# A hybrid diffusion layer: where the second gate's products, the token blocks and the last columns stand in the order of work

## The chip, the core and the metric

The kernel runs on one NeuronCore of a Trainium2 chip. Its engines are TensorE (PE: matrix products; PEld is its loading of weights), VectorE (DVE), ScalarE (ACT), GpSimd (POOL, here only an issuer of DMAs) and SyncE (SP, an issuer of DMAs). Each engine works its instructions off in program order and waits on semaphores. The metric is the device time of one execution in microseconds (us); lower is better.

## The reference, cut to what matters

One layer works on 512 tokens of width 2048 with a context of 256 tokens: modulation from a conditioning vector, a combined input projection, eight heads of a gated recurrence and eight heads of windowed attention, and then the part that the change touches:

```python
x = x + gt_m * (concat([hg_lat, at_lat]) @ w_out[l])
x = x + gt_f * swiglu(modulate(rms_norm(x, norm_ffn_g[l]), sh_f, sc_f), w_gate_up[l], w_down[l])
# swiglu(h): gate, up = split(h @ w_gate_up); return (silu(gate) * up) @ w_down     D_FF = 5632
# gt_f is one sixth of silu(c) @ w_mod[l] + b_mod[l]
```

All inputs are fp32. The result must keep nearly fp32 accuracy, so the kernel splits each operand into a high part (fp32r, rounded) and a low part (the rest), and forms high by high, high by low and low by high.

## The kernel before, in words

**Output projection.** `proj_a` multiplies eight blocks of 128 rows of the mixed heads (`mT`, split into two parts) with 512 columns of `w_out`; it holds one PSUM bank for each block of 128 tokens. Its loop `s` takes two row blocks at a time: four values of `s` (0, 2, 4, 6) for a pass, and for each token block six products of 512 columns. `Weights` loads the rows of `w_out` in 512 KB pieces on SP's queue (`wr`, three buffers) and splits them ahead on ACT (`wh`) and DVE (`wl`). After the last `s` of a token block, `add_gated` evacuates it: DVE multiplies by the gate (`tm`, one buffer), DVE adds to the residual `x1[j]`, ACT squares and sums. After token block 3, POOL stores `x1[j]` to `x1_d`. The second half of the heads has four passes j = 0 to 3 over the columns. Before, the last one (j = 3) is made as two passes over two token blocks each, and `w_out`'s last columns are loaded and split twice.

**The second gate.** `gt_f` needs `c @ w_mod` for 2048 columns. `gate_rows(k)` makes four products (column groups of the array) for the k-th of 16 blocks of rows (`gw`, 1 MB each, three buffers, loaded by POOL with `gate_load`). A caller's `before(s)` sets where they stand among the projection's products. Before: k = 0 to 3 in pass 2, 4 to 10 in the two halves of pass 3, 11 to 15 behind it. `est.strict` keeps all later instructions in program order on each engine; before, it starts ahead of pass 3.

**Norm and transposes.** Behind the projection DVE forms the reciprocal root mean square and `diag`, a diagonal matrix of it for each token block. `turn(s, h)` multiplies `x1` by `diag` on PE, which transposes and scales four blocks, into one auxiliary PSUM bank; ACT evacuates it with scale and shift into the block tile `xa[s]`.

**FFN by a seven-product scheme.** Each operand is cut in 2 by 2 blocks, and seven products of sums of blocks (Strassen's scheme in Winograd's form) take the place of eight. For the tokens, `a_sums` forms the four sums (`form_sums`), and `form_low` the low parts; the eight token sets of 14 KB per partition stay on chip (`asets`, tags a0 and a1, eight places each). For the weights, `steps` lists 264 steps: 176 up steps (22 groups of 256 columns by 8 steps) and 88 down steps (16 groups). Step i has 42 products (seven products, two halves, three of high and low). `st_load(i)` loads two 256 KB pieces into an `fx` tile, `st_sums` and `st_high` and `st_low` form sums, high parts (`fh`) and low parts (`fl`), each with three places. In iterations 0 to 5 `turn(i + 2, .)` also stands in the step, and before, `xa[s]` takes one of the three `fx` places.

**Evacuation and DRAM.** A group takes seven of the eight PSUM banks. `evac_up` forms the activations and splits them; POOL stores them to `sf_d` (two stores of 896 KB a group), and `reload` brings them back in pieces of 512 and 384 KB for the down steps, at most two per step before. `evac_down` forms four quarters of a 512 by 512 result; `move` stores partial results to `y_d` (adding there), and for the last round (`FIN`) adds `y_d` into the tile by DMA, multiplies by the gate on DVE, adds `x1_d` by DMA and stores to `out`. For the last columns (j = 3), `prepare(3)` does this to the earlier partial sum, and `done` finishes each quarter. `tail` and `moves` are lists of generators which are advanced by one `yield` per step.

Of the kernel before, what the change touches and what calls it, by code (L numbers as in the profile page):

```python
# [9 lines left out]
F32 = mybir.dt.float32  # L10
# [8 lines left out]
P = 128  # L19
D = 2048  # L20
KC = D // P
# [148 lines left out]
def tile_block(ctx: ExitStack, tc: tile.TileContext, x, c, ctx_in, c_ctx, w_mod, b_mod, norm_mix_g,  # L170
# [1254 lines left out]

    def a_sums(xx):
        dve.tensor_tensor(xx[:, 4:6, :], xx[:, 0:1, :].to_broadcast([P, 2, SC]), xx[:, 1:3, :], op=ALU.subtract)
        yield
        dve.tensor_tensor(xx[:, 6, :], xx[:, 5, :], xx[:, 1, :], op=ALU.subtract)
        dve.tensor_tensor(xx[:, 7, :], xx[:, 6, :], xx[:, 3, :], op=ALU.add)  # L1430

# [25 lines left out]
    for k in range(3):  # L1457
        gate_load(k)
    for j in range(3):
# [9 lines left out]
    est.strict = tc  # L1469
    for i in range(3):  # L1470
        st_load(i)
    last = add_gated(gp, 3, True)

    def before(s):
        gate_rows(4 + s // 2)
        if s == 2:
            st_sums(0)
            st_high(0)
        if s == 4:
            st_low(0)  # L1480
        if s == 6:
            st_sums(1)
            st_high(1)

    proj_a(ws, list(range(8)), mT, (0, 1), 512, last, before)

    def before(s):
        if s > 0:
            gate_rows(7 + s // 2)
        if s == 0:  # L1490
            st_low(1)

    proj_a(ws, list(range(8)), mT, (2, 3), 512, last, before)
    for k in range(11, KC):
        gate_rows(k)
# [18 lines left out]
    def turn(s, h):  # L1514

        if s >= 8:
            return
        if h == 0:
            new_set(s)
            xa[s] = est.tile(fx, [P, 8, SC], F32, "fx", "fx", 3)  # L1520
        kc = s + 8 * h
        pt = aux_bank()
        for n, t in enumerate((2, 3, 0, 1)):
            pe.matmul(pt[:, n * P:(n + 1) * P], x1[kc // 4][:, t, (kc % 4) * P:(kc % 4 + 1) * P], diag[:, t, :],
                      start=True, stop=True, skip_group_check=True)
        act.activation(xa[s][:, 2 * h:2 * h + 2, :], pt.rearrange("p (h t) -> p h t", h=2), AF.Identity,
                       bias=ab2[:, 1, kc:kc + 1], scale=ab2[:, 0, kc:kc + 1])

    def form_sums(s):
        if s < 8:  # L1530
            for _ in a_sums(xa[s]):
                pass
            act.activation(sets[s][0][:, 0:3, :], xa[s][:, 1:4, :], AF.Copy)
            act.activation(sets[s][0][:, 3:7, :], xa[s][:, 4:8, :], AF.Copy)

    def form_low(s):
        if s < 8:
            dve.tensor_tensor(sets[s][1], xa[s][:, 1:8, :], sets[s][0].bitcast(F32), op=ALU.subtract)

# [3 lines left out]
    def evac_up(g, banks):  # L1543

        p1, p2, p6, p7, q4, q5, p3 = banks
        e = est.tile(xg, [P, 4, 512], F32, "big", "big", 4)
        r, u0, t, u1 = (e[:, k, :] for k in range(4))
        act.activation(r, p1, AF.Copy)
        yield
        dve.tensor_tensor(u0, p2, r, op=ALU.add)  # L1550
        dve.tensor_tensor(r, p6, r, op=ALU.add)
        yield
        dve.tensor_tensor(t, r, p7, op=ALU.subtract)
        yield
# [11 lines left out]
        sums = a_sums(xx)  # L1566
# [6 lines left out]
        for i, (a, b) in enumerate(((0, 3), (3, 7))):  # L1573
# [11 lines left out]

    def prepare(j):

        gt = est.tile(fx, [P, 512], F32, "gtr", "gtr", 1)
        pool.dma_start(gt, gtf_d[0:1, 512 * j:512 * j + 512].to_broadcast([P, 512]))
        z = None  # L1590
        if j == 3:
            z = zs[0]
            dve.tensor_tensor(z, z, gt[:, None, :].to_broadcast([P, 4, 512]), op=ALU.mult)
            pool.dma_start(z, rows_of(x1_d, j), accum_op=ALU.add)
        prepared[j] = gt, z

    zs = []
    prepared = {}

    def evac_down(j, b, banks):  # L1600
        p1, p2, p6, p7, q4, q5, p3 = (hf(x) for x in banks)
        c = est.tile(xg, [P, 4, 512], F32, "big", "big", 4)
        c11, r, c21, t = (quad(c, h, n) for h, n in ((0, 1), (0, 0), (1, 1), (1, 0)))
        gt, z = prepared[j] if b == FIN else (None, None)

        def done(h, n):
            if z is not None:
                ck = quad(c, h, n)
                dve.tensor_tensor(ck, ck, gt[:, None, SC * n:SC * n + SC].to_broadcast([P, 2, SC]), op=ALU.mult)
                dve.tensor_tensor(ck, ck, quad(z, h, n), op=ALU.add)  # L1610
                sp_q.dma_start(quad(rows_of(out, j), h, n), ck)

        act.activation(r, p1, AF.Copy)
# [3 lines left out]
        yield  # L1617
        dve.tensor_tensor(t, r, p7, op=ALU.subtract)
        done(0, 1)
        yield  # L1620
        dve.tensor_tensor(c21, t, q4, op=ALU.add)
# [3 lines left out]
        done(1, 0)  # L1625
        yield
        dve.tensor_tensor(r, p3, r, op=ALU.add)
        done(0, 0)
        if z is None:
            moves.append(move(j, b, c, gt))  # L1630
        yield

    def move(j, b, c, gt):

        if b < FIN:
            for a in range(4):
# [10 lines left out]
        dve.tensor_tensor(c, c, gt[:, None, :].to_broadcast([P, 4, 512]), op=ALU.mult)  # L1647
        prepare(j + 1)
        pool.dma_start(c, rows_of(x1_d, j), accum_op=ALU.add)
# [5 lines left out]
    def run_step(i, hooks):  # L1655
        u = steps[i]
        ah, al = sets[u.a]
        if u.first:
            n = sum(v.last for v in steps[:i])
            u.banks = [(mm_bank if (n + k) % 2 == 0 else aux_bank)() for k in range(7)]  # L1660
        else:
            u.banks = steps[i - 1].banks
        for k, (fa, fb) in enumerate(PRODUCTS):
            if k in hooks:
                hooks[k]()
            for b in range(2):
                w = [v[:, fb, b * P:(b + 1) * P] if u.up else v[:, fb, :] for v in (u.hi, u.lo)]
                a = [v[:, fa, :] if u.up else v[:, fa, b * P:(b + 1) * P] for v in (ah, al)]
                mm3(u.banks[k][:, b * SC:(b + 1) * SC], *((w, a) if u.up else (a, w)), start=u.first, stop=u.last,
                    first=u.first and b == 0)  # L1670

# [32 lines left out]
    for i, u in enumerate(steps):  # L1704
# [25 lines left out]
        if not u.up and u.b == FIN and u.first:  # L1730
            if u.g == 0:
                prepare(0)
# [55 lines left out]
```

## Time and profile before

| what | value |
|---|---|
| time, median of 3 runs | 2645.55 us (2640.00 to 2646.84) |
| the profiled execution | 2641.55 us, span 2639.8 us |
| mean granted TensorE clock | 0.984 |
| PE busy | 2531.1 us (96%), 17239 instructions |
| DVE busy | 2105.6 us (80%) |
| ACT busy | 1110.5 us (42%) |
| POOL busy | 265.7 us (10%) |
| chain that ended last | PE 68%, DVE 11%, DMA 10%, issue 6% |

The chain is followed back from the last instruction to what released it. PE is busy nearly all of the span, so time is lost or saved in the stretches where it is not: the end of the output projection and the first FFN steps (about 1200 to 1316 us), the first down steps (about 2160 to 2260 us), and the end.

### The profile page before, as it was taken

To read this page: it belongs to the slowest core of one execution; us is meant where nothing else is said; L and a number is where in the kernel's file an instruction comes from. 1 tells how busy PE (TensorE), PEld (TensorE's weight loads), DVE (VectorE), ACT (ScalarE), POOL (GpSimd) and SP (SyncE) were. 2 spreads that over 40 slices of the span, in tenths; PEclk is the share of its full clock that TensorE was granted. 3 is DMA by queue.
4 is the path that set the end of the run, shared out by engine and by line. 5 is a ranking of instruction groups with operands and counts; after the bars stand their busy time and mean duration, and the time that the engine had idled before them with its cause. 6 is when DMAs were issued, how large, how long until landed. Compare 5 with 4: busy or idle time off the path is not lost.

```text
span 2639.8 us, 44545 instructions
## 1 busy us (share of the span) xinstructions
PE 2531.1 (96%) x17239; PEld 2282.7 (86%) x17239; DVE 2105.6 (80%) x3691; ACT 1110.5 (42%) x1801; POOL 265.7 (10%) x466
## 2 busy tenths in 40 slices
PE   7999999999999999997899999999999999999996
PEld 4579877878888887774899999999999998999996
DVE  4467968787788886544898899899998988888886
ACT  4245444446533333323544444444444443343332
POOL 0000010000010211101000000000000023222301
PEclk9999999999999999998999999999999999999998
DMA  9978767662323335655254544544545587787867
GB/s 348 322 231 270 242 212 240 218 218 62 96 83 106 101 114 185 208 207 215 75 160 138 160 146 146 160 142 150 164 128 160 159 265 264 223 245 225 233 179 190
DMA packets 303574, 487.80 MB, mean 185 GB/s; under 512 B 20225, under 2 KB 177058, under 8 KB 300546
## 3 DMA queue, kind: packets, MB, share of 16 engines
q1 hardware_dynamic: 249824, 334.57, 40.0%
q0 software_dynamic: 40160, 137.74, 17.0%
q10 hardware_dynamic: 13378, 12.65, 1.5%
q8 instruction: 135, 2.21, 0.3%
q14 instruction: 77, 0.63, 0.1%
HBM read 413.04 MB, written 71.84 MB: 184 GB/s over the span
## 4 chain that ended last, share of the span: by engine, by line
PE 68%; DVE 11%; DMA 10%; issue 6%; ACT 2%; POOL 1%; SPq 0%; DVEq 0%; ACTq 0%; POOLq 0%
PE mm L131 40%; PE aux L131 28%; DMA m_w<-in_w_mod_dram 3%; DVE big L131 2%; DVE m_acc L131 2%; DVE wl L131 2%; DVE fx L131 1%; DMA wr<-in_w_in_dram 1%; DMA fx<-in_w_down_dram 1%; DMA big<-x_d 1%; DVE fl L131 1%; DVE ce L131 1%; DMA gw<-in_w_mod_dram 1%; DVE a L131 1%; POOL rs_t L131 1%
## 5 line engine op out<-in xcount | busy, mean ns | idle before, releaser
L131 ACT ACTIVATE fh<-fx 128x768 fp32r<-128x768 f32 (+1 forms) x528 | 500.2, 952 | 734.5 <-DVE fx L131 209.8
L131 DVE TENSOR_TENSOR fl<-fx,fh 128x1792 fp32r<-128x1792 f32 (+2 forms) x333 | 543.8, 1635 | 36.3 <-ACT fh L131 34.6
L131 PE MATMUL mm<-a,fh 128*128 128x256 f32 x2464 | 467.2, 283 | 4.8 <-DVE a L131 2.6
L131 PE MATMUL aux<-a,fh 128*128 128x256 f32 x2464 | 466.9, 283 | 1.4 <-ACT fx L131 0.9
L131 DVE TENSOR_TENSOR fx<-fx 128x256 f32<-128x256 f32 (+1 forms) x816 | 417.8, 512 | 57.9 <-DMA fx<-in_w_down_dram 26.3
L131 PEld LDWEIGHTS mm<-a,fh 128*128 128x128 f32 x2464 | 379.6, 188 | 6.0 <-DVE a L131 2.8
L131 PEld LDWEIGHTS aux<-a,fh 128*128 128x128 f32 x2464 | 379.5, 188 | 2.4 <-ACT fx L131 1.1
L131 ACT ACTIVATE wh<-wr 128x512 fp32r<-128x512 f32 x376 | 227.2, 628 | 306.5 <-PE mm L131 181.2
L131 PE MATMUL mm<-a,fl 128*128 128x256 f32 x1232 | 347.2, 282 | 0.0
L131 PE MATMUL aux<-a,fl 128*128 128x256 f32 x1232 | 347.2, 282 | 0.0
L131 DVE TENSOR_TENSOR wl<-wr,wh 128x512 fp32r<-128x512 f32 x376 | 251.2, 685 | 116.0 <-ACT wh L131 115.3
L131 PE MATMUL mm<-wh,hT 128*128 128x512 f32 x896 | 299.8, 404 | 3.8 <-ACT hT L131 2.9
L131 PE MATMUL aux<-fh,a 128*128 128x256 f32 x1232 | 265.5, 283 | 6.4 <-DVE big L131 6.3
L131 PE MATMUL mm<-fh,a 128*128 128x256 f32 x1232 | 265.9, 283 | 3.6 <-DVE big L131 3.5
L131 PE MATMUL mm<-hT,wh 128*128 128x512 f32 x768 | 247.8, 398 | 0.0
L131 PEld LDWEIGHTS aux<-a,fl 128*128 128x128 f32 x1232 | 232.1, 188 | 0.0
L131 PEld LDWEIGHTS mm<-a,fl 128*128 128x128 f32 x1232 | 232.0, 188 | 0.0
L131 PEld LDWEIGHTS mm<-wh,hT 128*128 128x128 f32 x896 | 170.3, 190 | 55.7 <-issue 8.6
L131 PEld LDWEIGHTS aux<-fh,a 128*128 128x128 f32 x1232 | 209.7, 190 | 8.4 <-DVE big L131 7.1
L131 PEld LDWEIGHTS mm<-fh,a 128*128 128x128 f32 x1232 | 210.1, 190 | 4.9 <-issue 2.2
L131 PE MATMUL mm<-wh,mT 128*128 128x512 f32 x512 | 171.4, 406 | 10.7 <-DVE gsig L131 4.0
L131 PE MATMUL mm<-wl,hT 128*128 128x512 f32 x448 | 179.5, 401 | 0.3 <-DVE wl L131 0.3
(280 smaller groups left out, 4088.6 us busy)
## 6 DMA issues: line engine op xcount, KB each, us to landing
fx<-in_w_gate_up_dram SPq DMA_DIRECT2D x352, 256.0 KB, 3.3
wr<-in_w_in_dram SPq DMA_DIRECT2D x144, 512.0 KB, 4.5
m_w<-in_w_mod_dram SPq DMA_DIRECT2D x96, 512.0 KB, 4.7
fx<-in_w_down_dram SPq DMA_DIRECT2D x176, 256.0 KB, 6.7
sf_d<-big POOLq DMA_DIRECT2D x44, 896.0 KB, 5.9
ring<-in_w_mod_dram SPq DMA_DIRECT2D x64, 512.0 KB, 8.9
a<-sf_d POOLq DMA_DIRECT2D x44, 512.0 KB, 11.7
wr<-in_w_out_dram SPq DMA_DIRECT2D x36, 512.0 KB, 4.5
```

What stands on the lines that cost most here:

```text
L131: r = f(*a, **k)
```

## The change

The three `for j` passes and the two half passes become four equal passes; `weave` spreads gate products 0 to 12 over passes 1 to 3 and leaves 13 to 15 behind them; the first weights are loaded in pass 1 and formed in passes 2 and 3; program order is kept from pass 1 on. The block tiles of the first six token sets take places of the set pool in place of `fx`'s. The stores to `sf_d` and `y_d` are issued one step later. `reload` takes two pieces at even steps and one at odd ones. The earlier partial sum of the last columns is prepared by `rest()` from the step after group 2's first of the last round. The last two steps go product by product, and `evac_last` finishes the quarters.

```diff
-        for j in (0, 1, 2, 3, 3) if half else range(4):
+        for j in range(4):
             ws.add(w_out, mix_order[8 * half:8 * half + 8], 512 * j, 512, 2)
...
+    def weave(j, s):
+        if j == 1 and s == 6:
+            for i in range(3):
+                st_load(i)
+        for k in {(1, 0): (0,), (1, 2): (1,), (1, 4): (2,), (1, 6): (3,), (2, 0): (4,), (2, 2): (5,), (2, 4): (6,),
+                  (2, 6): (7,), (3, 0): (8,), (3, 2): (9, 10), (3, 4): (11,), (3, 6): (12,)}.get((j, s), ()):
+            gate_rows(k)
+        for (jj, ss), f, i in (((2, 4), st_sums, 0), ((2, 4), st_high, 0), ((2, 6), st_low, 0), ((3, 0), st_sums, 1),
+                               ((3, 0), st_high, 1), ((3, 2), st_low, 1)):
+            if (jj, ss) == (j, s):
+                f(i)
+    for j in range(4):
         def before(s):
             if j == 0:
                 upto(s + 4)
-            if j == 2:
-                gate_rows(s // 2)
-            if s == 4:
+            weave(j, s)
+            if s == 4 and j < 3:
                 load_gate(gp, j + 1)
+        if j == 1:
+            est.strict = tc
         proj_a(ws, list(range(8)), mT, NT, 512, add_gated(gp, j, True), before)
...
-    proj_a(ws, list(range(8)), mT, (0, 1), 512, last, before)
...
-    proj_a(ws, list(range(8)), mT, (2, 3), 512, last, before)
-    for k in range(11, KC):
+    for k in range(13, KC):
         gate_rows(k)
...
-            xa[s] = est.tile(fx, [P, 8, SC], F32, "fx", "fx", 3)
+            if s < 6:
+                xa[s] = (est.tile(asets, [P, SC], F32, "a1", "xa0", 8), est.tile(asets, [P, 7, SC], F32, "a0", "xa", 8))
+            else:
+                xx = est.tile(fx, [P, 8, SC], F32, "fx", "fx", 3)
+                xa[s] = xx[:, 0, :], xx[:, 1:8, :]
...
-        act.activation(xa[s][:, 2 * h:2 * h + 2, :], pt.rearrange("p (h t) -> p h t", h=2), AF.Identity,
-                       bias=ab2[:, 1, kc:kc + 1], scale=ab2[:, 0, kc:kc + 1])
+        if h == 0:
+            act.activation(x0, pt[:, :SC], AF.Identity, **ab)
+            act.activation(xx[:, 0, :], pt[:, SC:], AF.Identity, **ab)
+        else:
+            act.activation(xx[:, 1:3, :], pt.rearrange("p (h t) -> p h t", h=2), AF.Identity, **ab)
...
+        moves.append(spill(g, hl))
+    def spill(g, hl):
+        yield
+        for i in range(2):
             pool.dma_start(sf_d[2 * g + i].bitcast(F32).rearrange("f p n -> p f n"), hl[i].bitcast(F32))
-            yield
+        yield
...
+    def rest():
+        z = est.tile(xg, [P, 4, 512], F32, "big", "big", 4)
+        pool.dma_start(z, rows_of(y_d, 3))
+        gate_cols(est.tile(asets, [P, 512], F32, "a0", "gt3", 8), 3)
+        yield
+        yield
+        dve.tensor_tensor(z, z, gts[3][:, None, :].to_broadcast([P, 4, 512]), op=ALU.mult)
+        pool.dma_start(z, rows_of(x1_d, 3), accum_op=ALU.add)
+        zs.append(z)
+        yield
...
         if b < FIN:
+            yield
             for a in range(4):
...
-        prepare(j + 1)
+        if j < 2:
+            gate_cols(est.tile(fx, [P, 512], F32, "gtr", "gtr", 1), j + 1)
...
+        if i == len(steps) - 2:
+            return
         for k, (fa, fb) in enumerate(PRODUCTS):
...
+            for u in steps[-2:] if i == len(steps) - 1 else steps[i:i + 1]:
+                for b in range(2):
...
-        for _ in range(2):
+        for _ in range(2 - i % 2):
...
+        if i == len(steps) - 1:
+            evac_last(u.banks)
+            break
...
-        st_low(i + 2, not tail and not g)
+        st_low(i + 2, i >= 8 and not tail and not g)
...
         if not u.up and u.b == FIN and u.first:
...
-            if u.g == 3:
-                zs.append(est.tile(xg, [P, 4, 512], F32, "big", "big", 4))
-                pool.dma_start(zs[0], rows_of(y_d, 3))
+            if u.g == 2:
+                moves.append(rest())
```

## Rows read from the trace of the kernel before

**Rows 1.** Windows: busy PE, PEld, DVE, ACT, POOL (instructions), PEclk, DMA share, GB/s.

```profile
1220.00:1240.00 20.00, 11.64 (x66) 3.99 (x64) 6.12 (x21) 1.45 (x4) 2.35 (x4) 0.75 0.71 258
...
1260.00:1280.00 20.00, 15.72 (x129) 15.30 (x130) 15.86 (x22) 11.20 (x14) 0.00 (x0) 1.00 0.27 80
...
1320.00:1340.00 20.00, 20.00 (x169) 20.00 (x168) 19.06 (x24) 10.11 (x11) 1.52 (x2) 1.00 0.52 168
```

**Rows 2.** Chain that ended last: start us, length us, what; from four places.

```profile
1157.25 1.00 PE aux L131 x8
1158.24 5.67 PE mm L131 x24
...
1317.63 0.72 PE mm L131 x6
...
2153.97 10.36 DMA fx<-in_w_down_dram
```

**Rows 3.** Timeline of PE, 1220 to 1250: start, length, operation, [idle before <-releaser].

```profile
1224.78 0.39 PE L131 MATMUL mm<-wh,mT 128*128 128x512 f32 x1
...
1235.89 1.94 PE L131 MATMUL aux<-gw,c_pad 128*32 128x512 f32 x8 [7.03 <-DMA gw<-in_w_mod_dram]
...
1240.24 4.73 PE L131 MATMUL aux<-diag,x 128*128 128x128 f32 x40
```

**Rows 4.** Timeline of DVE: evacuation of a token block, and the norm's end.

```profile
1184.40 0.69 DVE L131 TENSOR_TENSOR tm<-mm,gt_c 128x512 f32<-128x512 f32 x1 [0.85 <-ACT tm L131]
...
1226.11 0.69 DVE L131 TENSOR_TENSOR tm<-mm,gt_c 128x512 f32<-128x512 f32 x1 [0.85 <-ACT tm L131]
...
1231.58 0.69 DVE L131 TENSOR_TENSOR diag<-ident,rs_y 128x512 f32<-128x512 f32 x1
```

**Rows 5.** Timeline, a transposing step (DVE, ACT, PE, DVE) and PE one later.

```profile
1267.01 2.02 DVE L131 TENSOR_TENSOR a<-fx,a 128x1792 fp32r<-128x1792 f32 x1
...
1269.13 0.78 ACT L131 ACTIVATE fx<-aux,ab 128x512 f32<-128x512 f32 x1 [2.21 <-DVE a L131]
...
1269.96 1.16 PE L131 MATMUL aux<-diag,x 128*128 128x128 f32 x8 [1.41 <-ACT fx L131]
...
1271.96 1.61 DVE L131 TENSOR_TENSOR fx<-fx 128x512 f32<-128x512 f32 x3 [1.42 <-ACT fx L131]
...
1278.44 1.16 PE L131 MATMUL aux<-diag,x 128*128 128x128 f32 x8 [1.40 <-ACT fx L131]
```

**Rows 6.** Waits from 1190 to 1320: total us, times, longest us.

```profile
PE aux L131 <- ACT fx L131: 8.9, 6, 2.4
```

**Rows 7.** Waits from 2150 to 2300: total us, times, longest us.

```profile
PE aux L131 <- DVE big L131: 6.3, 4, 2.4
...
PE mm L131 <- DVE big L131: 3.5, 4, 2.0
```

**Rows 8.** Timeline of POOL's DMA issues in the first down steps.

```profile
2152.10 1.01 POOL L131 DMA_DIRECT2D sf_d<-big  x1 [9.23 <-DVE big L131]
2153.11 6.05 POOL L131 DMA_DIRECT2D a<-sf_d  x8
```

**Rows 9.** Timelines of POOL, DVE and PE at the end.

```profile
2600.44 1.30 POOL L131 DMA_DIRECT2D big<-y_d  x1 [4.08 <-DVE big L131]
...
2609.90 2.29 DVE L131 TENSOR_TENSOR big<-big,gtr 128x2048 f32<-128x2048 f32 x1 [3.47 <-DMA big<-y_d]
...
2616.70 0.28 PE L131 MATMUL aux<-fh,a 128*128 128x256 f32 x1
...
2618.61 2.63 POOL L131 DMA_DIRECT2D big<-x_d  x2 [5.56 <-DVE big L131]
...
2632.49 0.79 POOL L131 DMA_DIRECT2D out_dram<-big  x1 [11.25 <-DMA big<-x_d]
```

**Rows 10.** DMA from 1130 to 1245: GB/s in 40 slices; packets, volume, mean.

```profile
GB/s 24 158 12 218 354 211 143 71 153 32 174 390 422 262 287 274 358 366 407 75 10 311 365 406 387 418 404 243 15 148 219 228 211 291 188 299 430 177 6 3
DMA packets 8278, 26.31 MB, mean 229 GB/s; under 512 B 720, under 2 KB 2256, under 8 KB 6608
```

More of the change, by code (lines that the diff above doesn't have):

```diff
@@ L1458, in tile_block @@
         gate_load(k)
-    for j in range(3):
+    def weave(j, s):
[10 more added lines that the diff above has]
+    for j in range(4):
         def before(s):
@@ L1525, in turn @@
                       start=True, stop=True, skip_group_check=True)
-        act.activation(xa[s][:, 2 * h:2 * h + 2, :], pt.rearrange("p (h t) -> p h t", h=2), AF.Identity,
-                       bias=ab2[:, 1, kc:kc + 1], scale=ab2[:, 0, kc:kc + 1])
+        ab = dict(bias=ab2[:, 1, kc:kc + 1], scale=ab2[:, 0, kc:kc + 1])
+        x0, xx = xa[s]
+        if h == 0:
[3 more added lines that the diff above has]
+            act.activation(xx[:, 1:3, :], pt.rearrange("p (h t) -> p h t", h=2), AF.Identity, **ab)
     def form_sums(s):
         if s < 8:
-            for _ in a_sums(xa[s]):
+            for _ in a_sums(*xa[s]):
                 pass
-            act.activation(sets[s][0][:, 0:3, :], xa[s][:, 1:4, :], AF.Copy)
-            act.activation(sets[s][0][:, 3:7, :], xa[s][:, 4:8, :], AF.Copy)
+            act.activation(sets[s][0][:, 0:3, :], xa[s][1][:, 0:3, :], AF.Copy)
+            act.activation(sets[s][0][:, 3:7, :], xa[s][1][:, 3:7, :], AF.Copy)
     def form_low(s):
         if s < 8:
-            dve.tensor_tensor(sets[s][1], xa[s][:, 1:8, :], sets[s][0].bitcast(F32), op=ALU.subtract)
+            dve.tensor_tensor(sets[s][1], xa[s][1], sets[s][0].bitcast(F32), op=ALU.subtract)
     def hf(bank):
@@ L1565, in evac_up @@
         dve.tensor_tensor(xx[:, 1:4:2, :], hf(r), hf(u0), op=ALU.mult)
-        sums = a_sums(xx)
+        sums = a_sums(xx[:, 0, :], xx[:, 1:8, :])
         next(sums)
@@ L1572, in evac_up @@
         yield
-        for i, (a, b) in enumerate(((0, 3), (3, 7))):
+        for a, b in ((0, 3), (3, 7)):
             dve.tensor_tensor(hl[1][:, a:b, :], xx[:, 1 + a:1 + b, :], hl[0].bitcast(F32)[:, a:b, :],
                               op=ALU.subtract)
+            yield
[3 more added lines that the diff above has]
+        for i in range(2):
             pool.dma_start(sf_d[2 * g + i].bitcast(F32).rearrange("f p n -> p f n"), hl[i].bitcast(F32))
-            yield
+        yield
     def rows_of(d, j):
@@ L1584, in quad, with gate_cols, parts_of @@
         return c[:, 2 * h:2 * h + 2, SC * n:SC * n + SC]
[L1586 to L1598, printed above, removed]
+    def gate_cols(t, j):
+        pool.dma_start(t, gtf_d[0:1, 512 * j:512 * j + 512].to_broadcast([P, 512]))
+        gts[j] = t
+    def rest():
[8 more added lines that the diff above has]
+        yield
+    gts, zs = {}, []
+    def parts_of(c):
+        return [quad(c, h, n) for h, n in ((0, 1), (0, 0), (1, 1), (1, 0))]
     def evac_down(j, b, banks):
@@ L1602, in evac_down @@
         c = est.tile(xg, [P, 4, 512], F32, "big", "big", 4)
[L1603 to L1611, printed above, removed]
+        c11, r, c21, t = parts_of(c)
         act.activation(r, p1, AF.Copy)
@@ L1618, in evac_down, with evac_last, done @@
         dve.tensor_tensor(t, r, p7, op=ALU.subtract)
+        yield
+        dve.tensor_tensor(c21, t, q4, op=ALU.add)
+        dve.tensor_tensor(t, q5, t, op=ALU.subtract)
+        dve.tensor_tensor(r, q5, r, op=ALU.subtract)
+        yield
+        dve.tensor_tensor(r, p3, r, op=ALU.add)
+        moves.append(move(j, b, c))
+        yield
+    def evac_last(banks):
+        p1, p2, p6, p7, q4, q5, p3 = (hf(x) for x in banks)
+        c = est.tile(xg, [P, 4, 512], F32, "big", "big", 4)
+        c11, r, c21, t = parts_of(c)
+        def done(h, n):
+            ck = quad(c, h, n)
+            dve.tensor_tensor(ck, ck, gts[3][:, None, SC * n:SC * n + SC].to_broadcast([P, 2, SC]), op=ALU.mult)
+            dve.tensor_tensor(ck, ck, quad(zs[0], h, n), op=ALU.add)
+            sp_q.dma_start(quad(rows_of(out, 3), h, n), ck)
+        act.activation(r, p1, AF.Copy)
+        dve.tensor_tensor(c11, p2, r, op=ALU.add)
         done(0, 1)
-        yield
+        dve.tensor_tensor(r, p6, r, op=ALU.add)
+        dve.tensor_tensor(t, r, p7, op=ALU.subtract)
         dve.tensor_tensor(c21, t, q4, op=ALU.add)
@@ L1656, in run_step @@
         u = steps[i]
-        ah, al = sets[u.a]
         if u.first:
@@ L1665, in run_step @@
                 hooks[k]()
[L1666 to L1670, printed above, removed]
+            for u in steps[-2:] if i == len(steps) - 1 else steps[i:i + 1]:
+                for b in range(2):
+                    w = [v[:, fb, b * P:(b + 1) * P] if u.up else v[:, fb, :] for v in (u.hi, u.lo)]
+                    a = [v[:, fa, :] if u.up else v[:, fa, b * P:(b + 1) * P] for v in sets[u.a]]
+                    mm3(u.banks[k][:, b * SC:(b + 1) * SC], *((w, a) if u.up else (a, w)), start=u.first,
+                        stop=u.last, first=u.first and b == 0)
     uses = {}
```

38 lines of the change are left out of this document (8 added, 30 removed).

## The prediction

> **What bounds the kernel now.** I read the windows first, in stretches of 50 and then 20 us, since PE is busy 96% of the span and only the stretches where it is not can pay. Three fall out. From 1220 to 1240 us PE has 11.64 of 20 us and a mean granted clock of 0.75; from 1260 to 1280 it has 15.72; from 1320 on it is full [rows 1]. The chain of waits tells what a full stretch costs: one `s` of a pass with four token blocks takes 5.67 us, a gate row 1.00, and six FFN products 0.72, so the 42 of a step take 5.04 us [rows 2]. Third, PE's timeline shows why the first stretch is empty: the projection's last product ends at 1225.2 us, a gate row behind it starts after 7.03 us of waiting for its 1 MB load, and the transposes start only at 1240.24 [rows 3]. DVE does not hold them: `diag` is done at 1232.3, and the last token block's evacuation started at 1226.1; within a pass one starts every 2.26 us (from the one at 1182.14 to that at 1184.40), because ACT gives `tm` back late [rows 4]. Fourth, the step with transposes turns in a ring of four: `form_low` of the set before ends on DVE, then ACT may write the shared `fx` place, then PE gets the one free bank for the second transposes (waits 1.41 us), then ACT, then DVE forms the sums; from one such wait to the next are 8.48 us [rows 5], and the six waits of this kind make 8.9 us [rows 6]. In the first down steps PE waits for DVE's evacuation, 9.8 us in all [rows 7]; DVE itself was late because a weight load took 10.36 us [rows 2], and that load met a burst: POOL stood 9.23 us at a store to `sf_d` and then issued eight reloads in 6.05 us [rows 8]. At the end PE is done at 2617.0, but the group before is multiplied by its gate at 2609.9, after its `y_d` addition; then come the last gate columns and the old partial sum's product, at 2618.6 the two additions of `x1_d`, and at 2632.5 the last 1 MB store, which sets the end at 2639.8 [rows 9].
>
> **Term 1, the passes.** Pass 2 began with its gate row at 1157.25 [rows 2], so pass 1 began 4 x 5.67 earlier, at 1134.6. Three passes of 12 values of `s` with 13 gate rows take 12 x 5.67 + 13 x 1.00 = 81.0 us and end at 1215.6. Before they ended at 1225.2 with 11 rows in them, so 11.6 us were waits or half-speed products. What goes: four loads of 512 KB, eight splits on ACT and on DVE (not on the bound; with two token blocks per `s` they came twice as often as PE could use them). What is added: the three weight loads, their sums and parts (DVE about 3.6 us a step, from 1.6 us of sums and 2.0 of low parts [rows 5]), now behind a full `s` of 6.67 us and covered by splits that are made two values of `s` ahead. Program order from pass 1 on puts four evacuations (4 x 2.26 = 9.0 us, starting when the first block is ready) ahead of the next pass's splits; these end some 6 us into the pass and are needed after 5.67 + 1.00 + half a microsecond. Tight, so I leave 2 us of waits: the end is 1217.6, gain 7.6. Bounds: 9.6 if none, nothing if all the old waits come back.
>
> The stretch's loads are the test of it. Before, 26.31 MB moved in 115 us, mean 229 GB/s, with slices of 366 to 430 GB/s [rows 10]. The new 81 us need 26.3 less 2.1 (the second load of the last columns) and 1.05 (the fourth `x1_d` store falls behind), plus 1.05 for weights loaded early as their places come free: 24.2 MB, 299 GB/s. The Trainium skill ("DMA: Bandwidth & Descriptors", Specifications) gives an HBM limit per core of about 358 GB/s; by it alone the 24.2 MB would take 68 us, so the passes would still be PE's. This case's slices go beyond the figure, and the measurement decides.
>
> **Term 2, the hold before the transposes.** Before: 1240.2 - 1225.2 = 15.0 us [rows 3]. After: blocks are ready every 5.67 / 4 = 1.42 us but evacuated every 2.26, so the last starts at -3 x 1.42 + 3 x 2.26 = 2.5 us behind the end; from there to `diag`'s end was 1232.3 - 1226.1 = 6.2 us [rows 4]: 8.7. Three gate rows (3 us) lie inside it, and the last one's load is issued 5.7 us before the end, so even a 9 us landing is covered. Gain 6.3. Without that cover it is what it was: bound 0.
>
> **Term 3, a cold start.** PE now idles some 5.7 us between gate row 15 and the first transposes. After 7.03 us of idling a gate row took 1.94 us instead of 1.00 [rows 2, 3], the lower of the two clock levels; those slow rows stood ahead of the transposes, whose 40 products then took 4.73 us at the upper one [rows 3]. If half of them run slow that costs 2.4 us, on the path, for ACT needs all four banks before the first high parts. The evacuation in two instructions where there was one of 0.78 us [rows 5] costs between nothing and 0.78 each; I take 0.4 for the ones on the path. Loss 2.8; bounds 0 and 4.7 + 0.8.
>
> **Term 4, the transposing steps.** Own places remove the wait of ACT for `form_low`, so the first transposes' bank is free before PE comes back for it. Without the 1.41 us a step is 8.48 - 1.41 = 7.07 us of PE work; DVE's is the same period less its own wait of 1.42, 7.06 [rows 5]. They balance, so nearly all of the 8.9 us goes [rows 6]; I take 8. Bounds: 3 (DVE and ACT bind at 8 us a step) and 8.9. The last two blocks still use `fx`, in steps where a free place is waiting two us earlier.
>
> **Term 5, the down steps.** The later stores and the slower reload change the order in POOL's queue, not what is moved. POOL is not paced by steps: behind the last store it waits for, it issues everything up to the next. Counting the new list, eleven pieces (not eight) run ahead of the two `sf_d` stores, and behind these come two stores and seven pieces, 4.6 MB, where before one store and eight pieces came, 4.6 MB as well [rows 8]. So the burst stays, and with it DVE's lateness. I take 1 us gain; bounds 9.8 us and a few of clock gained [rows 7], and 5 lost (more pieces ahead of the first weights). Reloads come at the latest five steps, 25 us, before use, hence cost nothing; the held `big` places come free about a step before the next group needs them; the low part in one piece instead of two changes no path.
>
> **Term 6, the end.** `rest` takes the gate columns, the multiplication (2.29) and the first addition out of the end, to step 256. There DVE has 2.3 us more; queued behind are the product of group 1, the next sums and group 2's evacuation, so that chain is 2.3 us later. In the old trace's time: `y_d` addition issued at 2600.4 + 2.3, landing after 9.5, multiplied by 2614.5; the `x1_d` addition (as long as that of `y_d`, 9.5) and 0.3 of issue to 2624.3; the store, from issue to the span's end 7.3 as before, and 0.3 to 2631.9 [rows 9]. The last group is done earlier: 15 DVE instructions of 512 columns from 2614.5, each 0.69 [rows 4], reach 2624.9, and then only 256 KB are left to store, against 1 MB. So the order by product earns nothing by itself: cover is that chain. Gain 7.9, less 1 for weight loads that meet two additions at once: 7. Bounds 3 and 10.
>
> **Sum.** 7.6 + 6.3 - 2.8 + 8 + 1 + 7 = 27.1 us. The profiled execution took 2641.55 us, so 2614.5; it lies 4.0 below the median of 2645.55, from which the sum gives 2618.4. I predict 2616 between them.
>
> **Rivals.** (a) The moved stores do cure the down steps, all of 9.8 us: 2607. For it: POOL's 9.23 us stand and the eight loads behind it; against: the count of term 5. (b) The loads bind the passes. At the old mean of 229 GB/s 24.2 MB take 106 us: the end comes at 1240, term 1 turns from 7.6 gained to 15 lost, and the time is 2616 + 22.6 = 2639; from about 220 GB/s downwards, 110 us, it is slower than before, 2645 and more. Against it: slices of 366 to 430 GB/s in the same stretch, and 20 us of lead for each load. At a mild form, 6 us of waits, 2622. (c) DVE or ACT binds the transposing steps at 8 us: 2621. (d) The clock stays low through all transposes, 4.7 in place of 2.4: 2618. The Trainium skill ("TensorE: Matmul & The Clock Gate", Part 1) says that the clock follows how busy PE was just before, which speaks against leaving PE without gate rows there; the 1.94 us row agrees. (e) The passes stay as late as they were and nothing else counts: within 0.3%.
>
> **Chances and range.** 0.3% (7.9 us) is about what a measurement of this kernel can tell from no change. Forecast 0.50; (a) 0.18; (b) 0.12, of which slower 0.04 and the same 0.03; (c) 0.10; (d) 0.07; (e) 0.03. Faster 0.90, same 0.06, slower 0.04. The range takes (a) with its clock and the upper bounds of terms 4 and 6 at the one end, 2599, and the mild form of (b) together with (c) and the lower bound of term 6 at the other, 2631.
>
> **What would show it.** Right: pass 3's last product near 1217, transposes near 1226, no PE wait of 1.41 us for ACT in steps of about 7.1 us, the full stretch beginning near 1290 instead of 1316, PE still waiting for DVE around the first down groups, and and PE's last product some 15 us before the end instead of 22.8, with the 1 MB store of group 2 as the last to land. Wrong: weight waits in passes 1 to 3, a step of 8 us or more, down steps without waits, or an end set by the last quarters.

## The result, and the profile after

The changed kernel takes 2615.01 us (median of 4 runs, 2612.90 to 2616.42) where the kernel before, run beside it, takes 2642.78 (2639.81 to 2646.84): ratio 0.9893, 95% interval 0.9875 to 0.9912. Forecast were 2616 us and faster. The profiled execution took 2616.11 us, span 2614.3.

Medians of two kernels that differ by 3 us can't be told apart here, but the spans can be cut where PE's timeline has a mark, and the pieces repeat far better. The table has the start of pass 1 (before it nothing was changed; for the old passes it is the first gate row less four values of `s`), the time from there to the second product of step 0 (the row with 2.60 us of waiting for DVE `a`; 2.62 before), from there to the end of the last product, and what follows it. The starts spread over 6.9 us, in code that all kernels share; within one version of a stretch, the second and third columns agree to about 1 us (1.5 with paced reloads), while the last one spreads from 11.8 to 14.8 us over the nine kernels that have the changed kernel's end. The lower twelve kernels are the experiments below. The kernel before took 2636.76 to 2642.78 us beside the different groups of them, so they are compared by the ratio and by the columns, not by their times.

| kernel | pass 1 starts | to step 0's second product | to the last product's end | behind it | ratio to before |
|---|---|---|---|---|---|
| before | 1134.6 | 114.2 | 1368.2 | 22.8 | |
| after | 1132.6 | 101.9 | 1365.0 | 14.8 | 0.9893 [0.9875, 0.9912] |
| u_passes | 1127.7 | 117.4 | 1364.9 | 13.1 | 0.9953 [0.9938, 0.9969] |
| u_places | 1131.7 | 99.8 | 1372.5 | 14.4 | 0.9913 [0.9896, 0.9929] |
| u_down | 1127.9 | 101.6 | 1364.6 | 11.8 | 0.9899 [0.9881, 0.9917] |
| u_end | 1128.8 | 101.7 | 1362.9 | 23.0 | 0.9930 [0.9915, 0.9945] |
| x_warm | 1130.7 | 101.0 | 1363.9 | 11.8 | 0.9893 [0.9876, 0.9910] |
| x_row | 1133.1 | 100.9 | 1364.9 | 13.6 | 0.9908 [0.9890, 0.9926] |
| x_row_warm | 1129.4 | 98.4 | 1363.9 | 12.1 | 0.9889 [0.9868, 0.9910] |
| x_paced | 1131.3 | 101.6 | 1357.6 | 13.0 | 0.9880 [0.9863, 0.9898] |
| x_end2 | 1132.3 | 101.8 | 1372.7 | 7.4 | 0.9911 [0.9896, 0.9926] |
| x_noorder | 1130.2 | 101.6 | 1364.2 | 14.5 | 0.9911 [0.9885, 0.9936] |
| x_best | 1131.2 | 98.4 | 1365.2 | 7.4 | 0.9881 [0.9866, 0.9896] |
| x_warm_paced | 1128.8 | 98.4 | 1359.1 | 12.2 | 0.9862 [0.9845, 0.9878] |

Of the 25.5 us between the two spans, 2.0 are the start's scatter, 12.3 lie in the first stretch, 3.2 in the second and 8.0 behind the last product.

The windows of the kernel after, with the columns of [rows 1]:

```profile
1220.00:1240.00 20.00, 12.87 (x67) 12.35 (x68) 10.65 (x21) 8.38 (x13) 1.95 (x4) 0.67 0.11 41
...
1260.00:1280.00 20.00, 18.23 (x154) 17.98 (x153) 17.93 (x24) 13.96 (x18) 0.00 (x0) 1.00 0.17 53
...
1320.00:1340.00 20.00, 20.00 (x169) 19.96 (x168) 16.64 (x22) 7.86 (x10) 1.01 (x1) 1.00 0.44 140
```

The transposing steps are now 91% full (18.23 of 20 us, 15.72 before). The chain that ended last shows passes at their floor and, later, two slow weight loads (15.10 and 11.93 us):

```profile
1186.96 5.67 PE mm L131 x24
1192.63 1.85 PE aux L131 x16
...
2117.95 15.10 DMA fx<-in_w_gate_up_dram
...
2138.24 11.93 DMA fx<-in_w_down_dram
```

The chain before had two at this place as well, the 10.36 us of [rows 2] and, ahead of it, one of 12.40:

```profile
2131.64 12.40 DMA fx<-in_w_gate_up_dram
```

The timelines of PE, DVE, POOL and ACT between the projection and the first FFN step:

```profile
1213.13 0.39 PE L131 MATMUL mm<-wh,mT 128*128 128x512 f32 x1
...
1222.54 7.10 PE L131 MATMUL aux<-diag,x 128*128 128x128 f32 x40 [6.31 <-issue]
...
1234.47 0.58 PE L131 MATMUL mm<-a,fh 128*128 128x256 f32 x1 [2.60 <-DVE a L131]
...
1216.28 0.69 DVE L131 TENSOR_TENSOR tm<-mm,gt_c 128x512 f32<-128x512 f32 x1 [0.85 <-PE aux L131]
...
1221.75 0.69 DVE L131 TENSOR_TENSOR diag<-ident,rs_y 128x512 f32<-128x512 f32 x1
...
1223.33 1.95 POOL L131 DMA_DIRECT2D gtf_d<-g_row  x4 [4.57 <-DVE g_row L131]
...
1227.41 3.27 ACT L131 ACTIVATE xa<-aux,ab 128x256 f32<-128x256 f32 x6 [8.90 <-DMA gtf_d<-g_row]
```

The projection ends 81.0 us after pass 1 began, and the transposes start 9.0 us later. Two things are new: the 40 transposes take 7.10 us (4.73 in [rows 3]), at a granted clock of 0.67 in that window, and ACT can write the first block only when four stores of the gates' sum `g_row` have landed. The new places for blocks lie on memory that `g_row` had.

A transposing step, by DVE's `form_low` and PE's one remaining wait, and PE's waits for evacuations from 2090 to 2300:

```profile
1251.48 2.02 DVE L131 TENSOR_TENSOR a<-xa,a 128x1792 fp32r<-128x1792 f32 x1
...
1258.40 2.02 DVE L131 TENSOR_TENSOR a<-xa,a 128x1792 fp32r<-128x1792 f32 x1
...
1275.41 1.16 PE L131 MATMUL aux<-diag,x 128*128 128x128 f32 x8 [1.76 <-ACT fx L131]
```

```profile
PE aux L131 <- DVE big L131: 5.7, 4, 4.3
...
PE mm L131 <- DVE big L131: 3.9, 3, 2.0
```

A step takes 6.92 us, and the one wait of the old kind belongs to block 7, which still uses `fx`. In the down steps 9.6 us of waits stand where 9.8 stood [rows 7]. The window begins earlier than that of [rows 7] because these steps now come some 16 us earlier; before, it holds the same 9.8. POOL's issues there, and POOL, DVE and PE at the end:

```profile
2136.39 1.00 POOL L131 DMA_DIRECT2D sf_d<-big  x1 [13.55 <-DVE big L131]
2137.39 4.57 POOL L131 DMA_DIRECT2D a<-sf_d  x6
...
2563.98 1.30 POOL L131 DMA_DIRECT2D big<-x_d  x1 [11.01 <-DVE big L131]
...
2566.83 1.27 POOL L131 DMA_DIRECT2D big<-x_d  x1
2582.65 0.80 POOL L131 DMA_DIRECT2D out_dram<-big  x1 [14.54 <-DMA big<-x_d]
2583.43 1.32 POOL L131 DMA_DIRECT2D big<-y_d  x1
...
2594.84 2.29 DVE L131 TENSOR_TENSOR big<-big,gtr 128x2048 f32<-128x2048 f32 x1 [5.50 <-DMA big<-y_d]
...
2599.24 0.28 PE L131 MATMUL aux<-fh,a 128*128 128x256 f32 x1
...
2606.96 0.79 POOL L131 DMA_DIRECT2D out_dram<-big  x1 [8.23 <-DMA big<-x_d]
```

The end is group 2's chain, read upwards: the 1 MB store at 2606.96 waits for the `x1` addition, that for DVE's product at 2594.84, that for the `y_d` addition, which POOL issued only at 2583.43, behind the store of group 1 for which it stood 14.54 us. Last, the DMA view of the passes, 1130 to 1215 us:

```profile
DMA packets 7876, 24.18 MB, mean 284 GB/s; under 512 B 576, under 2 KB 3136, under 8 KB 6208
```

### The profile page after: what moved, and what is told of

Read it like the earlier page. It is cut to its first block, busy times and chain, and to the rows that moved or that the text cites. A ratio compares the mean times of both kernels' runs of the same rounds, so it can differ in the third digit from the quotient of the medians.

```text
span 2614.3 us, 44525 instructions
## 1 busy us (share of the span) xinstructions
PE 2525.6 (97%) x17239; PEld 2284.1 (87%) x17239; DVE 2098.8 (80%) x3676; ACT 1106.5 (42%) x1801; POOL 265.1 (10%) x466
## 4 chain that ended last, share of the span: by engine, by line
PE 71%; DVE 11%; DMA 9%; issue 5%; ACT 2%; POOL 1%; SPq 0%; DVEq 0%; ACTq 0%; POOLq 0%
PE mm L131 42%; PE aux L131 29%; DMA m_w<-in_w_mod_dram 4%; DVE m_acc L131 2%; DVE fx L131 1%; DVE big L131 1%; DVE wl L131 1%; DMA wr<-in_w_in_dram 1%; DVE fl L131 1%; DVE ce L131 1%; DMA fx<-in_w_down_dram 1%; DMA fx<-in_w_gate_up_dram 1%; DVE a L131 1%; DMA io<-mix_d 0%; POOL rs_t L131 0%
## 5 line engine op out<-in xcount | busy, mean ns | idle before, releaser
L131 DVE TENSOR_TENSOR fx<-fx 128x256 f32<-128x256 f32 (+1 forms) x798 | 408.5, 512 | 52.7 <-DMA fx<-in_w_down_dram 26.0
L131 ACT ACTIVATE wh<-wr 128x512 fp32r<-128x512 f32 x368 | 221.6, 627 | 290.1 <-PE mm L131 153.8
L131 DVE TENSOR_TENSOR wl<-wr,wh 128x512 fp32r<-128x512 f32 x368 | 245.2, 685 | 101.4 <-ACT wh L131 100.6
L131 PE MATMUL aux<-fl,a 128*128 128x256 f32 x616 | 173.8, 282 | 0.0
## 6 DMA issues: line engine op xcount, KB each, us to landing
a<-sf_d POOLq DMA_DIRECT2D x44, 512.0 KB, 11.4
a<-sf_d POOLq DMA_DIRECT2D x44, 384.0 KB, 11.4
```

Source lines behind the costliest of these rows:

```text
L131: r = f(*a, **k)
```

## The experiments

**The four parts undone, one at a time.** Each kernel is the changed one with one part put back as the kernel before has it: u_passes the two half passes with the gate rows' places, the late loading of the first weights and program order only behind the third pass, u_places the blocks in `fx`, u_down the stores to `sf_d` and `y_d` and two reloads a step, u_end the old preparation of the last columns and the last two steps one after the other.

```diff
 u_passes
-        for j in range(4):
+        for j in (0, 1, 2, 3, 3) if half else range(4):
 u_places
-            if s < 6:
-                xa[s] = (est.tile(asets, ...), est.tile(asets, ...))
+            xa[s] = est.tile(fx, [P, 8, SC], F32, "fx", "fx", 3)
 u_down
-            yield
-        moves.append(spill(g, hl))
+            pool.dma_start(sf_d[2 * g + i]..., hl[i]...)
+            yield
...
-        for _ in range(2 - i % 2):
+        for _ in range(2):
 u_end
-            if u.g == 2:
-                moves.append(rest())
+            if u.g == 3:
+                zs.append(est.tile(xg, [P, 4, 512], F32, "big", "big", 4))
+                pool.dma_start(zs[0], rows_of(y_d, 3))
...
-            evac_last(u.banks)
```

> The changed kernel with the old passes: last columns in two half passes, the second gate's products as before with five behind the projection, program order only from there. Theory (terms 1 to 3): the projection ends 9 to 10 us later, the transposes start 15 instead of 9 us behind it, and the first transposes are warm again (4.7 instead of 7.1 us): 11 to 15 us in all, time 2626 to 2630. Rival (the old waits were the chip's DMA rate and would show in the one-pass form as well): less than 5 us.

> The changed kernel with the token blocks back in the fx places and their evacuation in one instruction. Theory (the ring of four waits, term 4): PE waits for ACT's evacuation again in six steps, some 8 us in all, against the one of 1.8 us that is left in the changed kernel; steps of 8.5 us again. But ACT's first evacuation then no longer waits for the store of the second gate (8.9 us of idling in the changed trace, behind memory that its new place shares), so some 2 us come back: time 4 to 7 us above the changed kernel's 2615.0, 2619 to 2622. Rival (DVE or ACT would bind these steps anyway): less than 2 us.

> The changed kernel with the stores to sf_d and y_d at their old steps and two reload pieces at each step again. Theory (term 5: the same bursts in another order): PE's waits for DVE's evacuation in the first down steps stay between 7 and 11 us (9.8 before, 9.0 after), and the time stays within 3 us of 2615.0. Rival (a) (the moved stores cure these waits, and something else hid it): 6 to 10 us more.

> The changed kernel with the old end: the last columns' old partial sum prepared behind the group before, the last two steps one after the other. Theory (term 6): PE's last product to the end of the span 22 to 23 us instead of 14.8, PE itself about 1 us earlier, time 2621 to 2623. Rival (the order by product is what shortens the end): with the order undone, PE's end to the last quarter's store alone would grow, and the time by 2 to 5 us only.

u_passes: 2625.55 us, and the first stretch 15.5 us longer than in the changed kernel, a little over the 11 to 15 expected. The transposes run fast again (the first 32 take 4.85 us), but the first step does not gain by it: from the transposes to the second product it still takes 11.7 us, for ACT still waits for the store of `g_row` (its first block at 1238.08, 16.54 us idle, ended by that store). Its PE timeline has the split's late high parts and the gate row's late load back:

```profile
1199.91 0.80 PE L131 MATMUL mm<-wh,mT 128*128 128x512 f32 x1 [2.39 <-ACT wh L131]
...
1229.10 1.93 PE L131 MATMUL aux<-gw,c_pad 128*32 128x512 f32 x8 [7.14 <-DMA gw<-in_w_mod_dram]
```

u_places: 2615.91 us. The ring is back, with steps of 8.42 us (DVE's rows) and a wait of 1.33 to 2.00 in each of four (6.0 us in all; some 8 in six were expected), 7.5 us in the second stretch. But the first stretch is 2.1 us shorter: ACT starts 2.1 us after PE's first transposes (1223.74 after 1221.65), with no store ahead of it. The columns give 5.4 us together, within the 4 to 7 expected; the intervals of the two ratios overlap.

```profile
1258.00 2.02 DVE L131 TENSOR_TENSOR a<-fx,a 128x1792 fp32r<-128x1792 f32 x1
...
1266.42 2.02 DVE L131 TENSOR_TENSOR a<-fx,a 128x1792 fp32r<-128x1792 f32 x1
...
1269.37 1.16 PE L131 MATMUL aux<-diag,x 128*128 128x128 f32 x8 [1.33 <-ACT fx L131]
```

u_down: 2610.73 us, and 1364.6 against 1365.0 us: the later stores and the slower reloads are worth nothing that shows. PE's waits from 2090 to 2300 are 8.4 us (5.9 and 2.5), within the 7 to 11 expected. POOL's burst is there in both (here eight reloads in 6.03 us at 2128.10).

u_end: 2619.45 us. Behind the last product 23.0 us are back, as expected, in the old form: DVE's product waits for the gate columns, and both additions of `x1` come after it.

```profile
2592.16 2.29 DVE L131 TENSOR_TENSOR big<-big,gtr 128x2048 f32<-128x2048 f32 x1 [3.75 <-DMA gtr<-gtf_d]
...
2594.89 2.62 POOL L131 DMA_DIRECT2D big<-x_d  x2 [5.62 <-DVE big L131]
2608.67 0.79 POOL L131 DMA_DIRECT2D out_dram<-big  x1 [11.16 <-DMA big<-x_d]
```

Its second stretch is 2.1 us shorter, so the new end costs PE something; rows name 0.68 and 0.50 us of waits for DVE at 2577 in the changed kernel and 0.50 at 2572 here, the rest is within what that column scatters.

**The first step: a slow clock, or the store?** x_warm adds six rows of products that nobody uses ahead of the transposes, x_row puts the gates' sum into a place of its own, x_row_warm does both.

```diff
 x_warm (behind gate row 15)
+    idle = aux_bank()
+    for n in range(6):
+        for j in range(4):
+            pe.matmul(idle[32 * j:32 * j + 32, :], c_pad[:, 15, :], w15[:, 512 * j:512 * j + 512], ...)
 x_row
-    dve.tensor_tensor(g_row, pg[0], g_row, op=ALU.add)
+    g_sum = est.tile(fx, [P, 512], F32, "fl", "g_sum", 3)
+    dve.tensor_tensor(g_sum, pg[0], g_row, op=ALU.add)
```

> The changed kernel with six more gate rows of idle products (into a bank that nothing reads) between the last gate row and the first transposes, so that PE idles less than 1 us there. Theory (cold start, and behind it a second wait that the prediction had not seen: ACT's first evacuation stands 8.9 us until the second gate's stores have landed, because its place shares memory with their source): the 40 transposing products take 4.7 us instead of 7.1, but ACT still starts at the same time, so that the first step begins at most 1 us earlier; time 2614 to 2615. Rival (the cold start alone holds the first step): 2.4 us earlier.

> The changed kernel with the second gate's sum formed in a free place for low parts, so that no token block's place shares memory with the source of its stores. Theory: ACT's first evacuation follows PE's first transposes at once (no wait of 8.9 us), and with the transposes still cold the first step begins 1 to 2 us earlier; time 2613 to 2614. Rival (the store's wait is hidden behind the cold transposes): no change of the first step.

> Both edits together. Theory: the two waits stand one behind the other and each hides part of the other, so that both together bring more than the sum of each: from the first transposes to the first step's second product 9 us instead of 11.9, the first step 3 us earlier, time 2612. Rival (they add up): the sum of the two single gains.

The times are 2610.09, 2613.86 and 2607.60 us, too near each other for their intervals; the stretch from the first transposes to step 0's second product decides: 11.9 us in the changed kernel, 11.0, 10.9 and 8.4 here. PE's timelines of x_warm and x_row with ACT's of x_row, then of x_row_warm:

```profile
1220.62 3.81 PE L131 MATMUL aux<-diag,x 128*128 128x128 f32 x32 [1.14 <-issue]
...
1225.65 1.16 PE L131 MATMUL aux<-diag,x 128*128 128x128 f32 x8 [1.22 <-ACT xa L131]
```

```profile
1223.09 7.19 PE L131 MATMUL aux<-diag,x 128*128 128x128 f32 x40 [6.29 <-issue]
...
1225.22 1.02 ACT L131 ACTIVATE xa<-aux,ab 128x256 f32<-128x256 f32 x2 [6.16 <-PE aux L131]
```

```profile
1219.37 4.70 PE L131 MATMUL aux<-diag,x 128*128 128x128 f32 x40 [1.15 <-issue]
...
1227.80 0.39 PE L131 MATMUL mm<-a,fh 128*128 128x256 f32 x1 [2.60 <-DVE a L131]
```

With idle products the transposes run fast, but PE then waits for a bank that ACT has not emptied. ACT starts only at 1224.57, 3.95 us after PE; its row names PE, but the chain of this run shows the store just ahead of it:

```profile
1222.86 1.53 DMA gtf_d<-g_row
```

With the store out of the way ACT starts 2.1 us after PE, but PE is slow. Each hides the other: without the store the slow clock costs 2.5 us (10.9 against 8.4), at the higher clock the store costs 2.6 (11.0 against 8.4). Both gone give 3.5 us, where the single ones add up to 1.9.

**The burst of reloads.** x_paced issues the reloads of the stationary sets on ACT's queue, each a step later than the place's last use, in the order of the steps instead of behind a waiting POOL.

```diff
-            if not parts or due[parts[0]] > i or uses[parts[0][0] - 8][-1] > i:
+            if not parts or due[parts[0]] > i or uses[parts[0][0] - 8][-1] >= i:
-            pool.dma_start(sets[n][k].bitcast(F32)[:, f0:f1, :],
+            act.dma_start(sets[n][k].bitcast(F32)[:, f0:f1, :],
```

> The changed kernel with the reloads issued from ACT's queue in place of POOL's, one step later than a set's last use, so that ACT's own work in each step spaces them out and no store stands ahead of them. Theory (term 5: bursts of reloads delay the weight loads, DVE comes late, PE waits for its evacuation and then runs at the lower clock level): no weight load over 8 us in the first down steps, PE's waits there fall from 9.0 to under 3 us, time 2603 to 2609. Rival (DVE's own work in these short groups is the bound, the loads come late for nothing): waits of 6 us or more stay, time above 2611. Second rival: issuing on ACT delays its evacuations, and the time rises.

2606.37 us, and the second stretch 7.4 us shorter (5.9 in x_warm_paced below). Three rows of PE's windows, 2100 to 2200 us (busy PE, granted clock, DMA share, GB/s), of after, u_down and x_paced, the DMA view's line for the down weights (time from issue to landing last), 2100 to 2160, of after and x_paced, and PE's waits in x_paced from 2090 to 2300:

```profile
2100.00:2200.00 100.00, 91.18 (x718) 0.93 0.75 254
```

```profile
2100.00:2200.00 100.00, 92.45 (x732) 0.95 0.87 295
```

```profile
2100.00:2200.00 100.00, 95.81 (x779) 0.97 0.81 270
```

```profile
fx<-in_w_down_dram SPq DMA_DIRECT2D x12, 256.0 KB, 9.1
```

```profile
fx<-in_w_down_dram SPq DMA_DIRECT2D x14, 256.0 KB, 4.3
```

```profile
PE aux L131 <- DVE big L131: 2.7, 2, 2.2
PE mm L131 <- DVE big L131: 2.4, 2, 2.0
```

Weight loads land in half the time, and PE's waits in the first down steps fall from 9.6 to 5.1 us. Less than 3 us were expected, so about half of the waits have another cause, which no run here shows. The rest of the gain stands in no wait; the granted clock over the 100 us is 0.97 in the place of 0.93. Which of the two edits does more was not separated. The Trainium skill ("DMA: Bandwidth & Descriptors", Issuing engines are not separate DMA queues) says that DMAs of all issuers run on the same 16 engines. It agrees with the long loads beside POOL's burst, and by it another queue as such would not make the loads faster; no run here tries it alone.

**The end.** x_end2 finishes the third group of columns in place as well, as the change does the fourth. x_noorder takes the order by product out of the last two steps and leaves all else.

```diff
 x_end2
+            if u.g == 1:
+                moves.append(rest(2, 3))
             if u.g == 2:
-                moves.append(rest())
+                moves.append(rest(3, 0))
...
+        own = j == 2 and b == FIN
+        if own:
+            done(c, j, 0, 1)
+            done(c, j, 1, 1)
 x_noorder
-        if i == len(steps) - 2:
-            return
...
-            for u in steps[-2:] if i == len(steps) - 1 else steps[i:i + 1]:
+            for u in steps[i:i + 1]:
```

> The change kept; in addition the third group of columns is finished by VectorE in place too, from a sum prepared beforehand (its gates loaded, the old partial sum read, multiplied and x1 added while the products run), and SyncE stores its quarters: no block load, no accumulating transfer and no add of 1 MB is left in the last 40 us except the second group's. Theory A (the 14.8 us behind the last product in the changed kernel are the accumulating chain of the third group, y_d added, then x_d added, then the out store on POOL's queue, and VectorE's last pass that waits 5.50 us for it): the end behind the last product falls to about 8 us, the time by 5 to 7 us. Rival B (VectorE's own last passes, some 8 us of rows, set the end, or its extra passes make the products wait): the end stays at 13 us or more and the time within 2 us of the changed kernel's.

> The change kept, but the last two down steps run one after the other again, each over all seven products, as before the change. Theory A (what is left behind the last product is set by the accumulating chain of the group of columns ahead, not by the last block's own evacuation): the time stays within 1 us of the changed kernel's, and the end behind the last product stays at 13 to 15 us, or shows the chain a little longer while the wait on it goes. Rival B (the order by product lets VectorE take the first products' sums while the last ones run, and is what won most of the end): the end behind the last product grows by 4 us or more and the time with it.

x_end2: 2613.08 us. The end behind the last product is 7.4 us as theory A has it, but the second stretch is 7.7 us longer, as B has it. DVE's and PE's timelines show the first piece of that:

```profile
2543.45 2.29 DVE L131 TENSOR_TENSOR big<-big,gt 128x2048 f32<-128x2048 f32 x1 [2.26 <-issue]
...
2547.91 0.44 PE L131 MATMUL aux<-fh,a 128*128 128x256 f32 x1 [3.71 <-DVE big L131]
```

The preparation falls between the pieces of the evacuation of the group before. DVE stands idle (the chain has the preparation's `y_d` load there, 14.58 us from 2527.81) and then multiplies, and PE waits 3.71 us; 1.04, 1.15 and 0.98 follow at 2580 to 2597. These make 6.9 us where the changed kernel has 1.2; the other 2 us were not traced. x_noorder: 2611.16 us and 14.5 us behind the last product, with the same chain on the same waits:

```profile
2591.11 2.29 DVE L131 TENSOR_TENSOR big<-big,gtr 128x2048 f32<-128x2048 f32 x1 [5.27 <-DMA big<-y_d]
...
2603.06 0.79 POOL L131 DMA_DIRECT2D out_dram<-big  x1 [8.07 <-DMA big<-x_d]
```

The 14.5 lie within the spread of the kernels that keep the order (11.8 to 14.8), so the order by product earns nothing that shows.

**Together.** x_best has the own place, the idle products, the paced reloads and x_end2's end; x_warm_paced leaves that end out.

> The change kept, with four additions: the gates' sum in a place of its own, six idle products ahead of the first transposes, the stationary reloads one step later on ScalarE's queue, and the third group of columns finished in place. If the parts add up: the first two gave 4.8 us together (ratio 0.9889 against 0.9893 or 0.9908 alone), the later reloads 5.7 us, the end 5 to 7 us, so 2595 to 2600 us where the changed kernel takes 2612 to 2615. If the late reloads or the extra passes of VectorE meet at the end (both fall in the down steps), the last two are worth less than 8 us together, and the time is 2600 us or more.

> The change kept, with three additions and without the third group's finish in place: the gates' sum in a place of its own, six idle products ahead of the first transposes, and the stationary reloads one step later on ScalarE's queue. Theory (the three act in stages far apart, 900 us, and each stands on the path that sets the end): the trace shows the first transposes to the second product in 8.4 us, from full blocks to the last product 1295.5 us, and 13 us behind the last product; the time is the sum, 4.8 + 5.7 us under the changed kernel, that is a ratio of 0.985 to 0.9865 to the kernel before, 2601 us where the changed kernel takes 2612. Rival (the late reloads' gain was the run's own scatter, as the 1303.0 to 1304.3 us from full blocks to the last product of other runs may be): that stretch is again 1301 us or more and the ratio 0.987 to 0.989.

x_best takes 2606.07 us, not the 2595 to 2600 of parts that add up: x_end2's end takes the paced reloads' gain back (1365.2 us in the second stretch). x_warm_paced takes 2601.24 (2600.24 to 2601.85), ratio 0.9862, within its expected band; both gains stand in their own columns of the table, 3.5 us in the first stretch and 5.9 in the second. Its interval meets those of x_paced, x_row_warm and x_best and just touches the changed kernel's, so that it is the fastest of them rests on the columns as well as on the ratio.

## Why the prediction was right

The total was forecast at 27.1 us. The spans differ by 25.5, of which 2.0 are scatter ahead of the change, so the change itself made 23.5 in these traces; the medians differ by 27.8. That the time lies within 1 us of 2616 is luck in part. Up to the full stretch the terms hold in sum, 19.1 forecast and 18.7 measured. Behind it 8 were forecast and 4.7 came, and the scatter of the start gave 2.0 back. Term by term:

- **Term 1**, forecast 7.6, measured 9.6: 90.6 us of passes before, 81.0 after, the upper bound. The 2 us of waits that I left for the evacuations did not come. 24.18 MB moved, as counted (24.2), at 284 GB/s over a slightly longer window, so rival (b) fell: in the passes no wait of PE for a weight is left.
- **Term 2**, forecast 6.3, measured 6.1: the hold is 9.0 us, by the evacuations' rhythm (the last one starts at 1216.28, 2.8 us behind the passes; forecast 2.5).
- **Term 3**, forecast -2.8, measured -3.4 (8.56 to 11.93 us). The size is near and the reasons are only half right: about half the transposes ran slow, as taken, 7.10 in place of 4.73 us (6.13 to 7.65 in the other runs that idle as long), but the store of `g_row` ahead of ACT was not seen. The two overlap: the slow clock by itself costs 2.5 us, close to the 2.4 taken, and the store puts 1.0 on top of it (x_warm, x_row and x_row_warm). The 0.4 for ACT's evacuation in two instructions does not show: with both causes gone this piece takes 8.4 us, 8.6 before. The Trainium skill ("TensorE: Matmul & The Clock Gate", Part 1) says that the clock follows how busy PE has been; the traces agree: the same 40 products took 7.10 us behind 6.31 us of idling and 4.70 behind 1.15. Rival (d), all 40 slow, is out.
- **Term 4**, forecast 8, measured 6.4 (from step 0's second product to the first full stretch 67.2 us before, 60.7 after) and 7.5 in u_places' column. Steps take 6.92 us (forecast 7.07), so rival (c) is out; what is missing is the wait of 1.76 us of block 7, which I had counted as gone.
- **Term 5**, forecast 1, is nothing: u_down shows it, and the waits stay (9.6 us after 9.8). Eleven pieces run ahead of the stores, as counted, and so rival (a) fell. Behind them come six and not the seven of the text; two stores and six pieces also make the 4.6 MB given there, which seven do not. Between the full stretch and the last product the changed kernel even loses 3.3 us to the one before, 1304.3 against 1301.0. u_end takes 1300.8 there, the kernels with the new end and POOL's reloads 1301.8 to 1305.0: the loss goes with the new end and is 1 to 4 us.
- **Term 6**, forecast 7 (7.9 behind the last product, less 1 ahead of it). Measured are 8.0 behind it, with the end that was described: group 2's `y_d` addition, product, `x1` addition, 1 MB store. The other kernels with this end would make it up to 11.0. With the 2.1 us that u_end saves ahead of it, 5.9 are left, so by these traces the 1 was too little. x_noorder agrees that the order by product earns nothing.

Two numbers of the prediction do not follow from its own sums. The full stretch would begin at 1296.9 (1316 less 7.6, 6.3 and 8, plus 2.8), not near 1290; it began at 1295.2, with a start 2.0 us earlier. And 110 us of passes in rival (b) give 2643, not 2645. Neither entered the forecast.

Undone one by one, the parts cost 15.4 us (passes), 5.4 (places) and -0.7 (stores) in the first two stretches, and the end 5.9 with what follows the last product: 26.0, against 23.5 for the whole. They are not independent, and the place where they meet is the first step: from the transposes to the second product are 8.6 us before, 9.8 in u_places and 11.7 in u_passes.

## What to carry to other kernels

Cut two traces at the same marks and compare the pieces: those up to the last product repeated to about 1 us where the starts of the same code differed by 7. Ask of each piece how far it repeats; the one behind the last product differed by 3. A tile that is put on memory of an earlier one waits for all that still reads that memory, a DMA store too; look at what lay there before. An issuer that stands at a store and then sends all it has queued can slow the loads of another queue; issue such transfers at their steps. Move work to the end's preparation only where the engine that does it has room.

## What the runs showed of the hardware that was not expected

Weight loads of the down steps took a median of 9.1 us beside POOL's burst and 4.3 us with the reloads issued step by step on ACT's queue. An accumulating DMA of 1 MB took 11.4 us from its issue to the next instruction (2583.43 to 2594.84) and 9.5 (2597.43 to 2606.96); two of them 2.85 us apart held the store behind them until 18.7 us after the first (2563.98 to 2582.65).
